# Layer 0 in another order (norm root, short convolution, diagonals), one more piece split ahead, and weight splits in steps of 1024 columns

## The chip, the cores and the metric

The kernel runs on one core of one Trainium2 chip. The metric is the time of one execution on the device in microseconds (us). PE is TensorE (matrix products), DVE is VectorE, ACT is ScalarE, POOL is GpSimd and SP is SyncE, whose queue issues the transfers (DMAs).

## What is computed

Two transformer-like blocks are applied to 256 tokens of 1024 channels, in float32. The first has an even layer (called layer 0 here) and an odd layer, the second a recurrent layer and a gated feed-forward. Layer 0, cut to what matters here:

```
z = h @ w_in;  va, vg, ga, xb, gb = split(z)
u   = depthwise_conv31(va * sigmoid(vg))          # "conv", 8 groups of 128 channels
y_a = silu(layernorm(u)) * silu(ga)
v   = depthwise_conv4(xb)                         # the short convolution
gr, gi = per-head products of v with w_r, w_i     # both directions
h_t = a_t * h_(t-1) + bx_t                        # linear recurrence, forward and backward
y_b = (h_forward + h_backward) * silu(gb)
x   = x + gate * (concat(y_a, y_b) @ w_out)
```

Each layer is preceded by a norm and by a scale and shift that come from a conditioning vector.

## The kernel before, in words

**Weights.** A piece of weights is a tile of 128 x 2048 floats (1 MB). SP loads it into one of 11 slots of the pool `w`. A product in float32 is made of three passes over two halves of lower precision: high x high, high x low and low x high (lines 365 to 367 with 256 or 512 tokens and columns, 413 to 415 with the weights as the moving side). ScalarE casts the high half of a piece (line 317) and VectorE subtracts it from the piece, which gives the low half (line 318). `halves` does that in steps of SW columns. `load_ahead(n_raw, n_split)` keeps 4 pieces loaded and LS = 2 split ahead of the one in use; where a layer's output rows take their last piece, `piece(last=True)` asks for LSB pieces instead, so LSB says how many pieces of the next layer are to be split before the residual and the norm between the layers.

**Order.** Layer 0's work is a table of names (`L0`): `glu`, `sh` and `cv` are the 31-tap convolution of a group, `xb`, `rb` and `gb` the recurrence's input, output rows and gate, `ga` and `co` the convolution's gate and output, `ln` its norm, `md` and `ml` the conditioning products (line 548, VectorE's sums line 507). The framework schedules the instructions of each engine from priorities which follow the order in which the code is written; on the chip each engine then runs its list strictly in order.

**Names used below.** `features(k)` (lines 771 to 774) makes the input of layer 0: VectorE xa, ScalarE hh, VectorE the low half. `shift` (line 901) copies a group's signal four times into the tile `four`, by four DMAs. `conv` makes a tile of diagonals `dg` on VectorE (line 908), which `order_after(..., tables["low"])` keeps behind the instruction held there, and multiplies `four` by it (line 915). `lru_in` makes the short convolution: ScalarE the third tap (j = 2, line 962), then VectorE three taps j = 0, 1, 3 for each of two heads q (line 968, tile `u`); the products of `u` with the gates' weights are line 372 (two of the four pieces xb use the three-pass form instead). ScalarE's gates, line 999 (`asq`) and VectorE's lines 996, 1000 and 1013 to 1019 (the scans) follow. `conv_norm` (lines 1024 to 1047) centres the convolution's result, sums its squares on TensorE (line 1042), and takes the root: VectorE line 445, POOL a power, VectorE and ScalarE two diagonals (lines 435 and 436), TensorE line 439, and a copy of it to `rsl`.

Of the kernel before, what the change touches and what calls it, by code (L numbers as in the profile page):

```python
# [8 lines left out]
F32 = mybir.dt.float32  # L9
# [3 lines left out]
ALU = mybir.AluOpType  # L13
# [4 lines left out]
MB = (6, 0)  # L18
MLATE = 0
TAIL = 400  # L20
LSB = 2
FENCE0 = -1
NT2 = 8
EARLY = (1, 1)
# [4 lines left out]
DIRECT = ('gv', 'so')  # L29
HOLD = ((), (), ())  # L30
LATE = [0, 2000, 600, 0]
SW = 512
SW_FROM = 0
START = [('w', 17), ('l', 4), ('x', 0), ('a', 0), ('y', 0), ('k', 0), ('w', 1), ('q', 0), ('w', 4), ('s', 0), ('f', 0), ('z', 0), ('r', 0), ('S', 0), ('a', 1), ('l', 2), ('k', 1), ('Z', 0), ('q', 1), ('f', 1), ('R', 0), ('a', 2), ('l', 2), ('r', 1), ('k', 2), ('q', 2), ('f', 2), ('s', 1), ('z', 1), ('R', 1), ('a', 3), ('l', 2), ('r', 2), ('k', 3), ('S', 1), ('Z', 1), ('q', 3), ('f', 3), ('R', 2), ('a', 4), ('l', 2), ('r', 3), ('k', 4), ('q', 4), ('f', 4), ('s', 2), ('z', 2), ('R', 3), ('a', 5), ('l', 2), ('r', 4), ('k', 5), ('S', 2), ('Z', 2), ('q', 5), ('f', 5), ('R', 4), ('a', 6), ('l', 2), ('r', 5), ('k', 6), ('q', 6), ('f', 6), ('s', 3), ('z', 3), ('R', 5), ('a', 7), ('l', 0), ('r', 6), ('k', 7), ('S', 3), ('Z', 3), ('q', 7), ('f', 7), ('R', 6), ('r', 7), ('R', 7), ('n', 1)]

# [12 lines left out]
]  # L48
# [42 lines left out]
T = 256  # L91
# [136 lines left out]
def build(tc, gates, wp, mp, vec, xT, cT, c2T, tok, cst, crow, out, dbg=None):  # L228
    nc = tc.nc
# [19 lines left out]
    def t1(name, shape=(P, T), dt=F32):  # L249
        return wk.tile(list(shape), dt, name=name, tag="t1", bufs=5)  # L250
# [246 lines left out]
    md = {}  # L497
# [218 lines left out]
    with ExitStack() as st0:  # L716
# [52 lines left out]
        def features(k):  # L769
            t = t1("xa")  # L770
            nc.vector.scalar_tensor_tensor(out=t, in0=X[:, k, :], scalar=A0[:, k, 0:1], in1=rsx, op0=ALU.mult, op1=ALU.mult)
            mod_shift(k)
            nc.scalar.activation(hx[0][:, k, :], t, AF.Identity, bias=S0[:, k, 0:1])
            nc.vector.scalar_tensor_tensor(out=hx[1][:, k, :], in0=t, scalar=S0[:, k, 0:1], in1=hx[0][:, k, :].bitcast(F32),
                                           op0=ALU.add, op1=ALU.subtract)

        def half_piece(s, g, low):

# [166 lines left out]
        def lru_in(m):  # L945

            gw = t4("gw", (P, 1024))
            nc.sync.dma_start(gw, gates[m])
            if m in GS:
                raw, gw = gw, [t4("gwh", (P, 1024), F32R), t4("gwl", (P, 1024), F32R)]  # L950
                split(*gw, raw)
            else:
                gw = [gw]
            pc = cut(piece(), k=KT)
            us, tiles = [], []
            bs = []
            for q in range(2):
                b = mm_bank()
                cols_both(b, pc, q)
                u = t2("u", (P, 2, T))  # L960
                h = 2 * m + q
                nc.scalar.activation(flat(u), b, AF.Identity, scale=v("ev_sconv_w", 16 + h), bias=v("ev_sconv_b", h))
                us.append(u)
                bs.append(b.rearrange("p (s t) -> p s t", s=2))
            for j in (0, 1, 3):
                o, i = (slice(2 - j, T), slice(0, T - 2 + j)) if j < 3 else (slice(0, T - 1), slice(1, T))
                for q in range(2):
                    nc.vector.scalar_tensor_tensor(out=us[q][:, :, o], in0=bs[q][:, :, i], scalar=v("ev_sconv_w", 8 * j + 2 * m + q),
                                                   in1=us[q][:, :, o], op0=ALU.mult, op1=ALU.add)
            for q in range(2):  # L970
                h = 2 * m + q
                us[q] = flat(us[q])
                rt, it, tt = (t4(n, (P, 2, 512)) for n in ("rt", "it", "tt"))
                tiles.append((rt, it, tt))
                up_ = [us[q]]
                if m in GS:
                    ut = t4("ut", (P, 2, 512), F32R)
                    up_ = [ut[:, i, :] for i in range(2)]
                    split(*up_, us[q])
                for d in range(2):  # L980
                    for w, (dst, bn) in enumerate(((rt, "ev_b_r"), (it, "ev_b_i"))):
                        g = side_bank()
                        o = (4 * q + 2 * d + w) * 128
                        mm_w(g, gw, up_, np.s_[:, o:o + 128], True, True)
                        act(dst[:, d, :], g, AF.Tanh, scale=0.5, bias=v(bn, 8 * d + h))
                for d in range(2):
                    act(tt[:, d, :], rt[:, d, :], AF.Tanh, scale=sp[:, 8 * d + h:8 * d + h + 1],
                        bias=sp[:, 8 * d + h:8 * d + h + 1])
            for q in range(2):
                h = 2 * m + q  # L990
                rt, it, tt = tiles[q]
                for d in range(2):
                    act(rt[:, d, :], rt[:, d, :], AF.Exp, scale=spn[:, 8 * d + h:8 * d + h + 1],
                        bias=spn[:, 8 * d + h:8 * d + h + 1])
                for d in range(2):
                    nc.vector.scalar_tensor_tensor(out=it[:, d, :], in0=it[:, d, :], scalar=1.0, in1=us[q],
                                                   op0=ALU.add, op1=ALU.mult)
                sq = t4("asq", (P, 2, 512))
                nc.scalar.activation(sq, rt, AF.Square)
                nc.vector.scalar_tensor_tensor(out=tt, in0=sq, scalar=1.0, in1=tt, op0=ALU.add, op1=ALU.mult)  # L1000
            lru[m] = tiles
# [22 lines left out]
        def conv_norm():  # L1024

            half = [cv[i // 2][:, 2 * (i % 2):2 * (i % 2) + 2, :] for i in range(4)]
            s4, s1 = t2("s4", (P, 2, T)), t1("s1")
            nc.vector.tensor_tensor(out=s4, in0=half[0], in1=half[1], op=ALU.add)
            for i in (2, 3):
                nc.vector.tensor_tensor(out=s4, in0=s4, in1=half[i], op=ALU.add)  # L1030
            nc.vector.tensor_tensor(out=s1, in0=s4[:, 0, :], in1=s4[:, 1, :], op=ALU.add)
            mu = ms_bank()
            nc.tensor.matmul(mu[:, 0:T], ones, s1, start=True, stop=True)
            va = ms_bank()
            for i in range(4):
                nc.vector.scalar_tensor_tensor(out=half[i], in0=mu[:, None, 0:T].to_broadcast([P, 2, T]), scalar=-1.0 / D, in1=half[i],
                                               op0=ALU.mult, op1=ALU.add)
                sq, s1 = t2("sq4", (P, 2, T)), t1("s1")
                nc.scalar.activation(sq, half[i], AF.Square)
                nc.vector.tensor_tensor(out=s1, in0=sq[:, 0, :], in1=sq[:, 1, :], op=ALU.add)  # L1040
                for j in range(2):
                    nc.tensor.matmul(va[:, j:j + 1], s1[:, 128 * j:128 * (j + 1)], ones[:, 0:1],
                                     start=i == 0 and j == 0, stop=i == 3 and j == 1)
            rsl = t1("rsl")
            nc.scalar.copy(rsl, rstd_of(va[:, 0:2], D, 1e-5))
            return rsl
# [17 lines left out]
        for name, m in L0:  # L1064
# [17 lines left out]
                ga_piece(m)  # L1082
            elif name == "ln":
                rsl = conv_norm()
            elif name == "co":
                conv_y[m] = conv_out(m, rsl)
            else:
# [484 lines left out]
```

## Time and profile before

| | |
|---|---|
| Time, median of 3 runs | 922.4 us (921.48 to 922.65) |
| The profiled execution | 922.77 us |
| Its span, first to last instruction | 920.6 us |
| PE busy | 896.4 us, 97% of the span |
| DVE busy | 673.2 us, 73% |
| ACT busy | 540.7 us, 59% |
| POOL busy | 14.6 us, 2% |

The span is what the trace shows; 2.2 us of the execution lie outside it. A busy share is an average over many stages, and an engine that is busy 73% of the time can still be the one that is waited for in one of them.

### The profile page before, as it was taken

What the parts mean: (1) busy time and instruction counts of PE and PEld (TensorE: products, weight loads), DVE (VectorE), ACT (ScalarE), POOL (GpSimd) and SP (SyncE); (2) the same over time, 40 slices, a digit from 0 to 9 for tenths busy, and PEclk for the clock granted to TensorE, in tenths of its full rate; (3) what the DMA queues carried; (4) which work ended last, traced back from release to release, by engine and by line L of the source; (5) the groups of instructions that cost most, each with busy time, mean ns of one, the idle gap of its engine ahead of it and who ended that gap; (6) DMA issues with size and microseconds to landing.
All of it is one profiled execution on the core that took longest, in us unless ns stands there. A gap on an engine that the chain in (4) does not pass through costs nothing.

```text
span 920.6 us, 16648 instructions
## 1 busy us (share of the span) xinstructions
PE 896.4 (97%) x6770; PEld 805.8 (88%) x6770; DVE 673.2 (73%) x1273; ACT 540.7 (59%) x986; POOL 14.6 (2%) x26
## 2 busy tenths in 40 slices
PE   8999999899999989999999999999999999999996
PEld 6876887586889889999999898999999999898896
DVE  3589696967776896968874544999688977756644
ACT  4444879686775555546573335972674865645542
POOL 1000000000000000000000000000000000000000
PEclk9999999999999989999999999999999999999999
DMA  9969484154667765674641752355666467555511
GB/s 365 416 218 366 157 302 152 61 206 137 244 246 303 296 225 201 224 235 163 255 138 61 302 188 92 138 184 205 240 225 247 150 218 251 205 183 184 183 46 46
DMA packets 32172, 190.05 MB, mean 206 GB/s; under 512 B 3584, under 2 KB 8064, under 8 KB 10976
## 3 DMA queue, kind: packets, MB, share of 16 engines
q1 hardware_dynamic: 31536, 186.50, 56.7%
q0 software_dynamic: 560, 2.49, 0.7%
q8 instruction: 53, 0.87, 0.4%
q14 instruction: 23, 0.19, 0.1%
HBM read 183.28 MB, written 1.05 MB: 200 GB/s over the span
## 4 chain that ended last, share of the span: by engine, by line
PE 87%; ACT 5%; DVE 5%; DMA 1%; issue 1%; POOL 0%; DVEq 0%; SPq 0%; POOLq 0%; ACTq 0%
PE mm L365 12%; PE mm L367 12%; PE mm L366 12%; PE mm L394 9%; PE acc L365 7%; PE acc L366 7%; PE acc L367 7%; PE mm L395 4%; PE acc L915 2%; PE acc L795 2%; PE ms L548 2%; PE acc L640 1%; PE ms L678 1%; ACT L300 1%; PE mm L413 1%; PE mm L414 1%
## 5 line engine op out<-in xcount | busy, mean ns | idle before, releaser
L318 DVE TENSOR_TENSOR w<-w 128x512 fp32r<-128x512 f32 x460 | 298.0, 684 | 81.2 <-ACT w L317 75.8
L317 ACT CAST w<-w 128x512 fp32r<-128x512 f32 x460 | 256.0, 618 | 100.0 <-PE mm L366 20.6
L367 PE MATMUL mm<-hh,w 128*128 128x256 f32 (+1 forms) x784 | 238.0, 304 | 2.9 <-DVE w L318 2.9
L365 PE MATMUL mm<-hh,w 128*128 128x256 f32 (+1 forms) x784 | 238.8, 305 | 1.0 <-ACT w L317 1.0
L366 PE MATMUL mm<-hh,w 128*128 128x256 f32 (+1 forms) x784 | 236.9, 302 | 0.0
L365 PEld LDWEIGHTS mm<-hh,w 128*128 128x128 f32 x784 | 149.5, 191 | 14.0 <-issue 5.1
L367 PEld LDWEIGHTS mm<-hh,w 128*128 128x128 f32 x784 | 149.2, 190 | 9.9 <-DVE w L318 3.5
L366 PEld LDWEIGHTS mm<-hh,w 128*128 128x128 f32 x784 | 149.5, 191 | 8.0 <-issue 2.3
L394 PE MATMUL mm<-hh,w 128*128 128x512 f32 x336 | 118.8, 397 | 0.0
L395 PE MATMUL mm<-hh,w 128*128 128x256 f32 x336 | 94.2, 281 | 0.0
L394 PEld LDWEIGHTS mm<-hh,w 128*128 128x128 f32 x336 | 63.2, 188 | 14.7
L395 PEld LDWEIGHTS mm<-hh,w 128*128 128x128 f32 x336 | 63.8, 190 | 0.0
L507 DVE SCALAR_TENSOR_TENSOR w<-w,crow 128x1024 f32<-128x1024 f32 x40 | 47.8, 1220 | 20.8 <-DMA w<-in_mp 20.7
L366 PE MATMUL acc<-fl,w 128*128 128x256 f32 x176 | 49.7, 283 | 0.0
L367 PE MATMUL acc<-fh,w 128*128 128x256 f32 x176 | 49.6, 283 | 0.0
L365 PE MATMUL acc<-fh,w 128*128 128x256 f32 x176 | 49.4, 284 | 0.0
L366 PE MATMUL acc<-yl,w 128*128 128x256 f32 x128 | 37.2, 290 | 0.0
L367 PE MATMUL acc<-yh,w 128*128 128x256 f32 x128 | 36.8, 288 | 0.0
L365 PE MATMUL acc<-yh,w 128*128 128x256 f32 x128 | 36.8, 287 | 0.0
L366 PE MATMUL acc<-zl,w 128*128 128x256 f32 x128 | 36.3, 284 | 0.0
L367 PE MATMUL acc<-zh,w 128*128 128x256 f32 x128 | 36.2, 283 | 0.0
L365 PE MATMUL acc<-zh,w 128*128 128x256 f32 x128 | 36.2, 283 | 0.0
(344 smaller groups left out, 1715.5 us busy)
## 6 DMA issues: line engine op xcount, KB each, us to landing
w<-in_wp SPq DMA_DIRECT2D x115, 1024.0 KB, 5.0
w<-in_mp SPq DMA_DIRECT2D x48, 1024.0 KB, 6.7
four<-up SPq DMA_DIRECT2D x32, 142.0 KB, 4.2
w<-in_wp SPq DMA_DIRECT2D x8, 512.0 KB, 10.7
gw<-in_gates SPq DMA_DIRECT2D x4, 512.0 KB, 4.9
X<-in_xT SPq DMA_DIRECT2D x1, 1024.0 KB, 5.0
ct<-in_cT SPq DMA_DIRECT2D x2, 512.0 KB, 9.3
crow<-in_crow SPq DMA_DIRECT2D x2, 512.0 KB, 10.7
```

The costliest lines, as they stand in the source:

```text
L300: i = nc.scalar.activation(out, in_, func, **kw).ins
L317: a = nc.scalar.copy(hi, src).ins
L318: return a, nc.vector.tensor_tensor(out=lo, in0=src, in1=hi.bitcast(F32), op=ALU.subtract).ins
L365: nc.tensor.matmul(o, wh, xh, start=start, stop=False)
L366: nc.tensor.matmul(o, wh, xl, start=False, stop=False)
L367: nc.tensor.matmul(o, wl, xh, start=False, stop=stop)
L394: nc.tensor.matmul(b, w[0][:, k, c], HH[:, :, 0, k, 0:T], start=k == 0, stop=False)
L395: nc.tensor.matmul(b[:, 0:T], w[1][:, k, c], HH[:, 0, 0, k, 0:T], start=False, stop=k == KT - 1)
L507: nc.vector.scalar_tensor_tensor(out=w[:, i, :], in0=w[:, i, :], scalar=1.0, in1=s, op0=ALU.mult, op1=ALU.mult, accum_out=o[:, 2 * c + i, :])
L548: nc.tensor.matmul(pm[32 * j:32 * (j + 1), :], s[:, k, :], w[:, 512 * j:512 * (j + 1)], start=c == 0, stop=c == chunks - 1)
L795: nc.tensor.matmul(acc_of(acc[g], i), w[wp_][:, k % 4, 128 * i:128 * (i + 1)], hx[hp][:, k, :], start=k == 0 and i % 2 == 0 and wp_ + hp = ...
L915: nc.tensor.matmul(b[32 * i:32 * (i + 1), 0:T], dg[:, j, i, :], four[:, i, o:o + T], start=j == 0, stop=j == n - 1)
```

## The change

Five edits, with no change to what is computed:

1. SW goes from 512 to 1024: each piece is split by two casts and two subtractions instead of four and four.
2. LSB goes from 2 to 3.
3. The root of the convolution's norm becomes a table entry of its own, `lb`, which stands behind `rb1` and `gb2`; `ln` keeps the centring and the sums of squares.
4. In the short convolution the loop over the heads q is now outside and the taps j inside, so all three taps of head 0 stand before those of head 1.
5. `tables["low"]` is now also set by the low halves of `features`, so the diagonals of the first convolution stand behind the last of them on VectorE.

```diff
-LSB = 2
+LSB = 3
...
-SW = 512
+SW = 1024
...
-    ('rb', 1), ('gb', 2), ('md', 1), ('xb', 3), ('md', 1), ('rb', 2), ('md', 1), ('gb', 3), ('ga', 1), ('ga', 0),
+    ('rb', 1), ('gb', 2), ('lb', 0), ('md', 1), ('xb', 3), ('md', 1), ('rb', 2), ('md', 1), ('gb', 3), ('ga', 1), ('ga', 0),
...
-            nc.vector.scalar_tensor_tensor(out=hx[1][:, k, :], in0=t, scalar=S0[:, k, 0:1], in1=hx[0][:, k, :].bitcast(F32),
-                                           op0=ALU.add, op1=ALU.subtract)
+            tables["low"] = nc.vector.scalar_tensor_tensor(out=hx[1][:, k, :], in0=t, scalar=S0[:, k, 0:1],
+                                                           in1=hx[0][:, k, :].bitcast(F32), op0=ALU.add, op1=ALU.subtract).ins
...
-            for j in (0, 1, 3):
-                o, i = (slice(2 - j, T), slice(0, T - 2 + j)) if j < 3 else (slice(0, T - 1), slice(1, T))
-                for q in range(2):
+            for q in range(2):
+                for j in (0, 1, 3):
+                    o, i = (slice(2 - j, T), slice(0, T - 2 + j)) if j < 3 else (slice(0, T - 1), slice(1, T))
...
+            return va
+
+        def conv_root(va):
             rsl = t1("rsl")
             nc.scalar.copy(rsl, rstd_of(va[:, 0:2], D, 1e-5))
             return rsl
...
+            elif name == "lb":
+                rsl = conv_root(rsl)
```

On VectorE, at the end of the features: the diagonals `dg_642` of the first convolution (`dg_638` after the change) and the last features' xa, hh. Before:

```order
L490 SCALAR_TENSOR_TENSOR A0_103<-ms_481,V_68,b1_101 128x2
L908 TENSOR_TENSOR dg_642<-C_72,V_68 128x896
L771 SCALAR_TENSOR_TENSOR xa_509<-X_70,A0_103,rs_161 128x256
L495 TENSOR_SCALAR S0_104<-ms_481,V_68 128x2
L847 MEMSET sm_575 128x16
L774 SCALAR_TENSOR_TENSOR hh_67<-xa_509,S0_104,hh_67 128x256
L318 TENSOR_TENSOR w_559<-w_550,w_558 128x512 x4
```

Now:

```order
L490 SCALAR_TENSOR_TENSOR A0_103<-ms_481,V_68,b1_101 128x2
L771 SCALAR_TENSOR_TENSOR xa_509<-X_70,A0_103,rs_161 128x256
L495 TENSOR_SCALAR S0_104<-ms_481,V_68 128x2
L847 MEMSET sm_571 128x16
L774 SCALAR_TENSOR_TENSOR hh_67<-xa_509,S0_104,hh_67 128x256
L908 TENSOR_TENSOR dg_638<-C_72,V_68 128x896
L318 TENSOR_TENSOR w_559<-w_550,w_558 128x1024 x2
```

The diagonals moved behind xa and the low half of hh, and the split of `w_559` has two steps in place of four.

On TensorE, where the fourth convolution (`acc_838`, now `acc_830`, with the tile `four_722`, now `four_718`) begins. The rows ahead of each fence's first are products of the piece `mm_979`, now `mm_967`. Before:

```order
L439 MATMUL ms_883<-dg_880,ones_73 128x128 x2
L548 MATMUL ms_920<-w_918,S_81 32x512
L915 MATMUL acc_838<-four_722,dg_836 32x256 x3
L548 MATMUL ms_920<-w_918,S_81 32x512 x3
L548 MATMUL ms_920<-w_961,S_81 32x512
```

Now:

```order
L915 MATMUL acc_830<-four_718,dg_828 32x256
L439 MATMUL ms_875<-dg_872,ones_73 128x128
L915 MATMUL acc_830<-four_718,dg_828 32x256
L439 MATMUL ms_875<-dg_872,ones_73 128x128
L548 MATMUL ms_912<-w_910,S_81 32x512
L915 MATMUL acc_830<-four_718,dg_828 32x256 x30
```

The convolution now begins ahead of the norm product of line 439, and its first two matmuls stand apart. Ahead of it, 17 matmuls of `mm_967` stand behind line 612's, where before 12 of `mm_979` did. Further up, the first convolution stood behind 50 matmuls of the two pieces before it, and stands behind 35 now.

On VectorE, at the short convolution of the third piece xb (`u_1813` before, `u_1773` after). `w_1975`, `w_2031` and, before, `w_2030` are low halves of pieces to come. Before:

```order
L1018 TENSOR_TENSOR hsum_1686<-tt_1565 128x256
L1019 TENSOR_TENSOR sb_1684<-sb_1684,hsum_1686 128x512
L922 SCALAR_TENSOR_TENSOR cv1_616<-up1_618,V_68,cv1_616 128x256 x2
L318 TENSOR_TENSOR yl_1699<-sb_1684,yh_1698 128x512
L922 SCALAR_TENSOR_TENSOR cv1_616<-up1_618,V_68,cv1_616 128x256
L968 SCALAR_TENSOR_TENSOR u_1813<-mm_1788,V_68,u_1813 128x2x254
L922 SCALAR_TENSOR_TENSOR cv1_616<-up1_618,V_68,cv1_616 128x256
L968 SCALAR_TENSOR_TENSOR u_1813<-mm_1788,V_68,u_1813 128x2x255 x2
L318 TENSOR_TENSOR w_2030<-w_1776,w_2029 128x512 x2
```

Now:

```order
L1018 TENSOR_TENSOR hsum_1650<-tt_1533 128x256
L922 SCALAR_TENSOR_TENSOR cv1_612<-up1_614,V_68,cv1_612 128x256
L1019 TENSOR_TENSOR sb_1648<-sb_1648,hsum_1650 128x512
L922 SCALAR_TENSOR_TENSOR cv1_612<-up1_614,V_68,cv1_612 128x256
L318 TENSOR_TENSOR w_1975<-w_1740,w_1974 128x1024
L318 TENSOR_TENSOR yl_1663<-sb_1648,yh_1662 128x512
L922 SCALAR_TENSOR_TENSOR cv1_612<-up1_614,V_68,cv1_612 128x256
L968 SCALAR_TENSOR_TENSOR u_1773<-mm_1748,V_68,u_1773 128x2x254
L968 SCALAR_TENSOR_TENSOR u_1773<-mm_1748,V_68,u_1773 128x2x255
L318 TENSOR_TENSOR w_2031<-w_1860,w_2030 128x1024
L968 SCALAR_TENSOR_TENSOR u_1773<-mm_1748,V_68,u_1773 128x2x255
```

Ahead of the third tap of head 0 there now stand one step of 1024 columns (`w_1975`) and, between the second tap and the third, a second one (`w_2031`); before, no step of a weight split stood between the scans and the third tap. Higher up, behind the second set of diagonals, one step of 1024 columns of `w_1975` takes the place of one of 512 of `w_1903`.

## Rows read from the trace of the kernel before

**Rows 1.** Page of the profile, part 1: busy time of each engine, its share, instructions.

```profile
PE 896.4 (97%) x6770; PEld 805.8 (88%) x6770; DVE 673.2 (73%) x1273; ACT 540.7 (59%) x986; POOL 14.6 (2%) x26
```

**Rows 2.** Busy time by stretch: from:to, length, PE, PEld, DVE, ACT, POOL, PEclk, DMA.

```profile
171.00:180.00 9.00, 6.59 (x25) 3.16 (x26) 8.77 (x15) 5.40 (x8) 1.93 (x3) 1.00 0.38 131
320.00:326.20 6.20, 4.13 (x33) 3.73 (x31) 6.20 (x12) 4.26 (x10) 0.00 (x0) 1.00 0.72 263
326.20:333.00 6.80, 6.18 (x29) 6.18 (x30) 6.80 (x12) 2.31 (x6) 0.00 (x0) 0.50 0.67 236
```

**Rows 3.** Groups by line and shape, VectorE: count, busy us, mean ns, idle before.

```profile
L318 DVE TENSOR_TENSOR w<-w 128x512 fp32r<-128x512 f32 x460 | 298.0, 684 | 81.2 <-ACT w L317 75.8 <-issue 2.0 <-PE acc L366 1.6
```

**Rows 4.** Groups by line and shape, ScalarE.

```profile
L317 ACT CAST w<-w 128x512 fp32r<-128x512 f32 x460 | 256.0, 618 | 100.0 <-PE mm L366 20.6 <-issue 18.1 <-PE mm L394 17.1
```

**Rows 5.** Line 786 (a low half made in 1024 columns): min/median/max ns.

```profile
L786 DVE TENSOR_TENSOR w<-w x9: 685/1225/1226, 14.8 to 45.6; 128x1024 fp32r<-128x1024 f32 x7, 128x512 fp32r<-128x512 f32 x2
```

**Rows 6.** Line 789 (a high half made in 1024 columns).

```profile
L789 ACT CAST w<-w x9: 620/1030/1053, 12.0 to 44.5; 128x1024 fp32r<-128x1024 f32 x7, 128x512 fp32r<-128x512 f32 x2
```

**Rows 7.** TensorE in order of time: start, us, line, tiles, [idle before].

```profile
49.09 1.15 PE L795 MATMUL acc<-hh,w 128*128 128x256 f32 x7 [1.13 <-ACT hh L773]
...
74.43 0.68 PE L439 MATMUL ms<-dg,ones 128*128 128x128 f32 x4 [0.30 <-DVE dg L435]
...
76.61 0.62 PE L915 MATMUL acc<-four,dg 128*32 128x256 f32 x2 [0.52 <-DMA four<-up]
...
170.60 0.39 PE L367 MATMUL mm<-hh,w 128*128 128x512 f32 x1
173.41 3.67 PE L372 MATMUL acc<-u,gw 128*128 128x512 f32 x8 [2.42 <-issue]
177.02 1.06 PE L548 MATMUL ms<-w,S 128*32 128x512 f32 x6
...
203.04 0.68 PE L439 MATMUL ms<-dg,ones 128*128 128x128 f32 x4 [1.02 <-DVE dg L435]
...
246.28 0.38 PE L367 MATMUL mm<-hh,w 128*128 128x256 f32 x1 [1.18 <-DVE w L318]
...
307.22 0.95 PE L556 MATMUL ms<-C,row 128*128 128x4 f32 x8
...
324.76 0.38 PE L365 MATMUL mm<-hh,w 128*128 128x256 f32 x1 [1.02 <-ACT w L317]
326.82 0.58 PE L367 MATMUL mm<-hh,w 128*128 128x256 f32 x1 [1.67 <-DVE w L318]
...
569.48 0.39 PE L414 MATMUL mm<-w,hh 128*128 128x256 f32 x1 [1.13 <-DVE w L318]
...
576.03 0.39 PE L414 MATMUL mm<-w,hh 128*128 128x256 f32 x1 [0.57 <-DVE w L318]
...
601.69 0.43 PE L1365 MATMUL acc<-lx,st 128*128 128x64 f32 x2 [0.49 <-DVE st L1376]
```

**Rows 8.** VectorE in order of time.

```profile
46.89 1.08 DVE L908 TENSOR_TENSOR dg<-C,V 128x896 f32<-128x896 f32 x1
47.89 0.48 DVE L771 SCALAR_TENSOR_TENSOR xa<-X,A,rs 128x256 f32<-128x256 f32 x1
...
155.25 1.23 DVE L1000 SCALAR_TENSOR_TENSOR tt<-asq,tt 128x1024 f32<-128x1024 f32 x1 [5.19 <-ACT asq L999]
...
157.52 1.22 DVE L1000 SCALAR_TENSOR_TENSOR tt<-asq,tt 128x1024 f32<-128x1024 f32 x1
...
160.26 1.22 DVE L1013 TENSOR_TENSOR it<-it,tt 128x1024 f32<-128x1024 f32 x1
...
171.79 1.52 DVE L968 SCALAR_TENSOR_TENSOR u<-mm,V,u 128x510 f32<-128x510 f32 x2
```

**Rows 9.** Transfer issues between 53.5 and 54.4 us: count, KB, us to landing.

```profile
four<-up SPq DMA_DIRECT2D x1, 142.0 KB, 2.8
```

**Rows 10.** Transfer issues between 69 and 69.9 us.

```profile
four<-up SPq DMA_DIRECT2D x2, 142.0 KB, 7.3
```

## The prediction

> **What bounds the kernel now.** I read the page first: TensorE is busy for 896 of 920.6 us, VectorE for 73% and ScalarE for 59% [rows 1]. So only what lets TensorE stand, or slows its clock, can move the end. Then the waits of TensorE in order of time, which give the places where another engine is late [rows 7]. They are few: 1.13 us for the last features, 0.30 and 0.52 us around the fourth convolution, 2.42 us for the short convolution of the third piece xb, 1.02 us for the root's diagonals, 1.18 us for a low half, 1.02 and 1.67 us at the start of layer 1, and in the recurrent layer 1.13, 0.57 and 0.49 us, with some smaller ones. Then the windows with the granted clock: from 326.2 to 333.0 us it is 0.50, that is 1.2 in place of 2.4 GHz, right behind the two waits of 2.69 us in sum; around the single wait of 2.42 us it stays at 1.00 [rows 2, 7]. TensorE's 6.18 busy us in that stretch would have been 3.09 at the full clock, so the slow stretch costs about 3.1 us.
>
> A difference under 0.2% (1.8 us) cannot be told from no change here.
>
> **Steps of 1024 columns.** 460 subtractions of 684 ns and 460 casts of 618 ns [rows 3, 4] become 230 each of 1225 and 1030 ns [rows 5, 6]. Instructions of one VectorE queue overlap by 0.08 us (the diagonals run from 46.89 for 1.08 us, the next starts at 47.89 [rows 8]), so in a full queue a step of 512 takes 0.60 us and one of 1024 takes 1.145: 0.06 us saved a pair, some 14 us over the kernel. On ScalarE it is at most 206 ns a pair. Neither engine ends the chain, so the price of this is zero where TensorE has work. It is not zero where TensorE waits for a half: the first columns of a piece come 0.54 us later, and an urgent instruction that finds a step ahead of it waits for 1.145 instead of 0.60 us.
>
> **The features and the convolutions (36 to 87 us).** The diagonals stood ahead of xa and took 1.00 us of the queue [rows 8]. Behind them stood xa, then ScalarE's hh, and TensorE waited 1.13 us for hh [rows 7]. Now they stand behind the low half of hh: -1.0. But the first convolution now comes after 35 matmuls in place of 50, 1.8 us earlier in its row, while its four copies land 2.8 us after issue each [rows 9] and can start only about 0.85 us earlier, since they need the sums that TensorE has just got earlier. The four land one after the other over 2.1 us; with eight matmuls between them to fill, I take a wait of 0.9. The fourth convolution's copies stand in SP's queue behind two loads of 1 MB; before, they landed 7.3 us after issue [rows 10], and TensorE waited 0.52 us for them and 0.30 just ahead for the norm's diagonals [rows 7]. The loads can be issued about 1.9 us earlier now, as the first convolution ends earlier. TensorE is about 1.3 us earlier at the sums of squares (line 612); then 17 matmuls follow where 12 did, and the norm product and line 548, which stood ahead of the convolution (1.7 us from 74.43 to the wait before 76.61), stand behind its first matmul. I estimate a wait of 1.5 in place of 0.82, and 0.2 for the single matmuls between products of another form. Sum: -1.0 + 0.9 + 0.7 + 0.2 = **+0.8**, between -1.1 (the copies land in time) and +2.0.
>
> **The short convolution of the third xb (155 to 178 us).** VectorE's queue is full here from 155.25 us to the end of the third tap (171.79 + 1.52 = 173.31), and TensorE starts the gates' products 0.1 us later, at 173.41 [rows 8, 7]. The heads' new order takes head 1's taps out from between head 0's, which gives little, as only head 0's stood there. What counts is what the scheduler put in. (a) The gate products of the second xb stand behind 12 more matmuls, so the last of them comes 1.4 us later; ScalarE was about 0.4 behind, so asq and line 1000 come 1.0 later than 155.25. (b) ScalarE has a cast of 1030 ns in place of 618 between the two asq: +0.4 for the second line 1000, which started at 157.52 [rows 4, 6, 8]. (c) The step of w_1975 behind the diagonals is 0.54 longer. So line 1013 begins 1.9 us later than 160.26. (d) From there the queue is the same up to the third tap, but for two steps of 1024 columns: +2.29. The third tap ends at about 173.31 + 1.9 + 2.3 = 177.5, and TensorE starts line 372 at 177.6. TensorE's own row ahead has three more products of line 548 (about 1.0 us by [rows 7], 177.02) and the four of line 556 (0.9 us for four); so it stands for about 177.6 - 172.0 - 0.85 = 4.75 us in place of 2.42: **+2.3**. The lower bound is 0 (ScalarE not later, and the steps filled by other waits), the upper 3.5.
>
> **The clock behind that wait.** Of the waits seen here, 2.42 us alone did not lower the granted clock, and 1.02 + 1.67 us with 0.3 of work between did [rows 2, 7]. A stand of 3.2 us, then line 556, then 1.5 us is longer than either. I take the lower clock at three chances in four, and its price as at 326.2 us: **+3.1**.
>
> The Trainium skill (TensorE: Matmul & The Clock Gate, section on HAM oscillation) says that a wait for data that is long enough lets the array's clock fall, so that the work behind it starts cold, and counts half of the cold time as lost. This trace agrees with the fall; by the page's half the 6.8 us cost 3.4 where the rows say 3.1, and the sum would be 0.3 higher in the case with one more fall.
>
> **The root (202 us).** Line 439 now stands behind all of `rb1` and of `gb2`, and one matmul more, while line 445 and the power start as soon as the sums are there. TensorE reaches it about as late as the diagonals are ready: the wait of 1.02 goes, **-1.0** (bounds -1.0 and +0.5).
>
> **Behind gb3 (245 us).** The low half that TensorE waited 1.18 us for stood on VectorE behind the scans; now both its steps stand ahead of line 1000. It goes; the next late thing is the recurrence's y for `rb3`, which then comes some 0.5 us after TensorE. **-0.7** (-1.2 to +0.5).
>
> **The start of layer 1 (323 us).** With LSB = 3, the second piece u is split before the residual, where VectorE and ScalarE stand. But the gate's piece that TensorE waited for is the third. Its cast is 1030 ns, so the wait of 1.02 becomes about 1.5; its low half still stands behind four sums of line 507 and ends its first step at about 325.6, where TensorE comes at 325.4: 1.75 in place of 2.69, **-1.0** (-2.5 to +1). A wait of that length did not lower the clock at 173 us, so I give six chances in ten that the 3.1 us of the slow stretch go too: **-3.1**. If they do not, the gain is only the 1.0.
>
> **The recurrent layer (566 to 605 us).** The first wait for a low half grows by 0.54, as its first step is 1024 columns. The wait of 0.57 for the last quarter of it goes, and 0.12 beside it. Then VectorE reaches the products `ke`, `kc` and the states later by two or three half steps each, and TensorE's row has been filled with more matmuls ahead: I estimate +0.5, +0.4 and +0.6 on waits that were 0.2 to 0.5 us [rows 7]. **+1.3**, between -0.7 and +2.5. Elsewhere (90 to 155, 340 to 540, from 660 on) TensorE has no wait that a half could shorten, and the queues of the other two engines have room.
>
> **The sum.** 0.8 + 2.3 - 1.0 - 0.7 - 1.0 + 1.3 = +1.7. The slow clock goes from 326 to 177 us: -3.1 + 3.1. Against the profiled execution's 922.77 that is 924.5; it ran 0.4 above the median, so I forecast **924.1** (own range 922 to 926).
>
> **Rivals.**
> 1. The slow clock comes at both places (the two waits at 324 us still suffice): 924.1 + 3.1 = 927.2. For it: the waits stay in the same pattern. Against: they are shorter.
> 2. It comes at neither: 921.0. For it: the stand at 172 us is cut in two by line 556. Against: 3.2 us alone is longer than anything that left the clock up here.
> 3. On the other side: `u` is not later. This is decided by whether TensorE has line 372's input by about 175.5 us: then it stands for 2.6 us, the clock stays, and the gains at 202, 245 and 324 us remain: 924.1 - 2.3 - 3.1 = 918.7. For it: (a) and (b) are estimates on ScalarE, whose queue had idle room just before 155.25 (VectorE stood 5.19 us [rows 8]). Against: the two steps of 1.145 us are in the row whatever ScalarE does.
> 4. The waits change places and nothing else, as the halves are made well ahead: 922.4.
>
> **Chances.** Forecast 0.40, rival 1 0.18, rival 2 0.17, rival 3 0.20, rival 4 0.05. With about 2 us of spread in each sum, faster by over 0.2% (below 920.6): 0.02 + 0 + 0.08 + 0.17 = 0.27; slower (above 924.2): 0.19 + 0.17 + 0.01 = 0.37; the rest, 0.36, within 0.2%. The range from 918 to 927.5 leaves out the outer parts of rivals 1 and 3.
>
> **What the profile after would show.** The wait of line 795 for hh near 47.7 us is under 0.2; line 915 has waits for `four` near 56 and 73 us; line 372 starts at 177 to 178 us behind 4 to 5 us of standing, with a granted clock of 0.50 behind it; line 439 near 204 us does not wait; the wait near 245 us is gone; at 324 us two waits sum to under 2 us and the clock is 1.00 from 326 to 333. The forecast is wrong if line 372 starts by 176 us, if 0.50 stands behind the waits at 324 us, or if a wait of over 1 us turns up in a stretch that I call free.

## The result and the profile after: slower by 1.2%

The changed kernel took **933.33 us** (median of 4 executions, 932.29 to 935.93), the kernel before 921.94 (4 executions beside it, 920.49 to 922.65). The ratio is 1.0121, with a 95% interval of 1.009 to 1.0152: slower by 11.4 us, where 924.1 was forecast with a range up to 927.5. The profiled execution took 935.93 us with a span of 934.2.

Of the page of the changed kernel, part 1, and from part 5 the groups of the two steps that the change doubled:

```profile
PE 905.2 (97%) x6770; PEld 806.4 (86%) x6770; DVE 660.0 (71%) x1043; ACT 519.4 (56%) x756; POOL 15.7 (2%) x26
...
L318 DVE TENSOR_TENSOR w<-w 128x1024 fp32r<-128x1024 f32 x230 | 277.2, 1220 | 99.9 <-ACT w L317 94.0
L317 ACT CAST w<-w 128x1024 fp32r<-128x1024 f32 x230 | 233.6, 1047 | 124.3 <-PE mm L366 28.4
```

Against [rows 1, 3, 4] the two engines that make the halves did get quicker: VectorE is busy for 13 us less and ScalarE for 21 us less. TensorE, which bounds the kernel, is busy for 9 us more with the same 6770 matmuls. So work was saved where time was to spare, and time was lost where there was none.

TensorE's waits in the changed kernel, summed by what it waited for (total, times, longest):

```profile
PE ms L556 <- ACT row L552: 3.5, 1, 3.5
PE ms L740 <- DVE xsq L735: 3.4, 1, 3.4
PE acc L915 <- DMA four<-up: 2.7, 3, 1.9
PE mm L414 <- DVE w L318: 1.7, 1, 1.7
PE mm L365 <- ACT w L317: 1.4, 1, 1.4
PE acc L365 <- ACT ut L317: 1.4, 1, 1.4
...
PE ms L1290 <- DVE ke L1342: 1.0, 1, 1.0
PE acc L795 <- ACT hh L773: 0.9, 2, 0.6
PE acc L372 <- DVE u L968: 0.7, 1, 0.7
PE acc L365 <- ACT yh L317: 0.5, 1, 0.5
```

Gone or smaller against [rows 7] are the waits for the last `hh` (1.13), for the root's diagonals (1.02), for the low half near 246 us (1.18) and the second of the two at the start of layer 1 (1.67). New or longer are those for `four` (2.7 in place of 0.52), for `ut` (1.4, none before), for `row` and `u` in one place (3.5 + 0.7 in place of 2.42), for `ke` and for `yh`. Line 414 waits for 1.7 us in one place, before in two (1.13 and 0.57).

The windows of the changed kernel (columns as in [rows 2]) show where the clock fell, that is went from 2.4 to 1.2 GHz (PEclk 0.50):

```profile
10.90:14.30 3.40, 3.40 (x22) 1.64 (x20) 0.00 (x0) 0.89 (x2) 0.00 (x0) 0.51 1.00 411
...
79.20:82.60 3.40, 3.40 (x12) 1.40 (x14) 0.19 (x1) 0.00 (x0) 0.00 (x0) 0.50 0.90 262
...
185.00:191.80 6.80, 6.10 (x14) 3.40 (x14) 5.38 (x9) 1.99 (x3) 1.42 (x3) 0.50 0.33 136
...
341.70:348.50 6.80, 6.80 (x60) 6.80 (x59) 6.80 (x9) 2.23 (x3) 0.00 (x0) 1.00 0.91 313
```

The slow stretch behind the waits of layer 1 [rows 2] is gone (layer 1 starts 15.5 us later here, so the last window is the same stretch of work). Three others have come: 3.4 us in the opening stretch, behind the wait for `xsq`; 3.4 us behind the wait for `four`; and 6.8 us behind the wait for `row`. TensorE in order of time at three of the new waits:

```profile
79.04 0.88 PE L915 MATMUL acc<-four,dg 128*32 128x256 f32 x2 [1.86 <-DMA four<-up]
...
148.55 0.50 PE L365 MATMUL acc<-ut,gwh 128*128 128x512 f32 x1 [1.44 <-ACT ut L317]
...
184.73 1.64 PE L556 MATMUL ms<-C,row 128*128 128x8 f32 x8 [3.48 <-ACT row L552]
187.07 1.22 PE L372 MATMUL acc<-u,gw 128*128 128x512 f32 x1 [0.70 <-DVE u L968]
```

VectorE, and under it ScalarE, of the changed kernel in order of time ahead of that last place:

```profile
180.57 0.69 DVE L1019 TENSOR_TENSOR sb<-sb,hsum 128x512 f32<-128x512 f32 x1
181.17 0.48 DVE L922 SCALAR_TENSOR_TENSOR cv<-up,V,cv 128x256 f32<-128x256 f32 x1
181.56 1.22 DVE L318 TENSOR_TENSOR w<-w 128x1024 fp32r<-128x1024 f32 x1
182.70 0.69 DVE L318 TENSOR_TENSOR yl<-sb,yh 128x512 fp32r<-128x512 f32 x1
183.30 0.48 DVE L922 SCALAR_TENSOR_TENSOR cv<-up,V,cv 128x256 f32<-128x256 f32 x1
183.70 1.53 DVE L968 SCALAR_TENSOR_TENSOR u<-mm,V,u 128x508 f32<-128x508 f32 x2
185.14 1.22 DVE L318 TENSOR_TENSOR w<-w 128x1024 fp32r<-128x1024 f32 x1
186.27 1.40 DVE L968 SCALAR_TENSOR_TENSOR u<-mm,V,u 128x510 f32<-128x510 f32 x2
```

```profile
181.29 0.62 ACT L317 CAST yh<-sb 128x512 fp32r<-128x512 f32 x1 [5.34 <-DVE sb L1019]
181.81 0.77 ACT L962 ACTIVATE u<-mm,V 128x512 f32<-128x512 f32 x1
182.49 1.03 ACT L317 CAST w<-w 128x1024 fp32r<-128x1024 f32 x1
183.42 0.78 ACT L962 ACTIVATE u<-mm,V 128x512 f32<-128x512 f32 x1
184.09 0.58 ACT L552 COPY row<-ms 128x512 f32<-128x512 f32 x1
```

This is how a full queue hands lateness on. VectorE reaches `sb` at 180.57; ScalarE stands for 5.34 us until it has it, because `yh` is next in its row; behind `yh` stand two `u`, a long cast and only then the copy of `row`, which TensorE's line 556 needs. On VectorE two steps of 1024 columns stand between `sb` and the third tap. TensorE is at line 556 at 181.25 and has `u` at 187.07.

Where the 13.6 us between the two spans lie, from the starts of the matmuls that have the same count on TensorE's row in both profiled executions (the order differs a little, so single places are right to some tenths):

| place on TensorE's row | after - before, us | forecast |
|---|---|---|
| opening stretch (wait for `xsq` 3.4 in place of 1.5, then a slow clock) | +2.9 | none |
| last features (`hh`) | -0.9 | -1.0 |
| the convolutions and the norm behind them | +5.3 | +1.8 |
| gates of the second xb (`ut`) | +2.1 | 0 |
| `row` and `u` of the third xb, with the clock behind them | +4.8 | +5.4 |
| root | -0.9 | -1.0 |
| behind gb3 | +2.2 | -0.7 |
| start of layer 1, with the clock behind it | -4.1 | -4.1 |
| rest of layer 1 | +0.8 | 0 |
| recurrent layer | +0.1 | +1.3 |
| everything behind it | +1.2 | 0 |

The opening stretch belongs to this execution more than to the change: the wait for `xsq` was 0.9 to 3.4 us over all the profiles, with 2.6 and 2.2 us in the first two kernels below.

### The profile page after: what moved, and what is told of

Its sections match the earlier page's. It is cut to its first block, busy times and chain, and to the rows that moved or that the text cites. A ratio compares the mean times of both kernels' runs of the same rounds, so it can differ in the third digit from the quotient of the medians.

```text
span 934.2 us, 16180 instructions
## 1 busy us (share of the span) xinstructions
PE 905.2 (97%) x6770; PEld 806.4 (86%) x6770; DVE 660.0 (71%) x1043; ACT 519.4 (56%) x756; POOL 15.7 (2%) x26
## 4 chain that ended last, share of the span: by engine, by line
PE 75%; DVE 12%; ACT 7%; issue 2%; DMA 2%; SPq 0%; POOL 0%; DVEq 0%; ACTq 0%; POOLq 0%
PE mm L365 10%; PE mm L367 10%; PE mm L366 10%; PE mm L394 8%; PE acc L365 6%; PE acc L366 6%; PE acc L367 6%; PE mm L395 4%; DVE w L318 2%; PE ms L548 2%; PE acc L795 2%; DMA four<-up 1%; ACT w L317 1%; PE acc L915 1%; ACT rt L300 1%
## 5 line engine op out<-in xcount | busy, mean ns | idle before, releaser
L318 DVE TENSOR_TENSOR w<-w 128x1024 fp32r<-128x1024 f32 x230 | 277.2, 1220 | 99.9 <-ACT w L317 94.0
L317 ACT CAST w<-w 128x1024 fp32r<-128x1024 f32 x230 | 233.6, 1047 | 124.3 <-PE mm L366 28.4
## 6 DMA issues: line engine op xcount, KB each, us to landing
crow<-in_crow SPq DMA_DIRECT2D x2, 512.0 KB, 10.2
```

The lines of the kernel that those rows point to most:

```text
L317: a = nc.scalar.copy(hi, src).ins
L318: return a, nc.vector.tensor_tensor(out=lo, in0=src, in1=hi.bitcast(F32), op=ALU.subtract).ins
```

## The experiments

My theory was that the doubled steps made the loss: VectorE and ScalarE work in order, so whatever stands behind a step of 1024 columns comes later, and the scheduler lays its rows out around the long steps. The rival was that the reordering of layer 0 made it (convolutions closer to their copies, root and taps in another place). A second rival was TensorE itself: the scheduler pulled apart line 548's groups of four matmuls, and each single one costs nearly as much as four.

### 1. Each part alone

The doubled steps in the kernel before, with nothing else:

```diff
-SW = 512
+SW = 1024
```

> The kernel before with weight splits in steps of 1024 columns and nothing else. Theory 1 (the long steps are the cause): VectorE and ScalarE run their lists in order, so an urgent instruction behind a step waits for 1.1 us instead of 0.6, and the scheduler lays the rows out for longer steps; nearly all of the loss of 11 us is here, +9 to +14 us, with waits of TensorE at the fourth convolution, at the gates of the second and third xb, and a granted clock of 0.50 behind at least one of them. Theory 2 (the new place of the root and of the diagonals is the cause): within 2 us of the kernel before.

The rest of the change, with the steps of 512 columns:

```diff
-SW = 1024
+SW = 512
```

> The changed kernel with the steps put back to 512 columns; the order of layer 0 and the third piece split ahead stay. Theory 1: faster than the kernel before by 1 to 5 us, since the waits at the last features and at the root go (1.0 us each) and the start of layer 1 gains what the third piece gives. Theory 2: slower by 6 to 11 us.

The kernel before with three pieces of layer 1 split ahead, alone:

```diff
-LSB = 2
+LSB = 3
```

> The kernel before with three pieces split ahead of a layer's end and nothing else. If the pieces split ahead are what took the two waits at 324 us down in the changed kernel, they shrink here too and the granted clock stays at 1.00 from 326 to 333 us: -2 to -5 us. If it was the longer step that did it (fewer steps behind the sums of line 507), the waits stay as before and the time within 1 us.

The kernel before with the root's own entry in the list, the taps by head, and the diagonals behind the low half, but with LSB = 2 and 512 columns (edits 3, 4 and 5 of the change, shortened here):

```diff
-    ('rb', 1), ('gb', 2), ('md', 1), ('xb', 3),
+    ('rb', 1), ('gb', 2), ('lb', 0), ('md', 1), ('xb', 3),
...
-            nc.vector.scalar_tensor_tensor(out=hx[1][:, k, :], in0=t, scalar=S0[:, k, 0:1], in1=hx[0][:, k, :].bitcast(F32),
+            tables["low"] = nc.vector.scalar_tensor_tensor(out=hx[1][:, k, :], in0=t, scalar=S0[:, k, 0:1],
...
-            for j in (0, 1, 3):
+            for q in range(2):
+                for j in (0, 1, 3):
```

> The kernel before with the new place of the root, the short convolution by heads and the diagonals behind the features; steps of 512, two pieces ahead. Theory 1: the waits of 1.13 us at the last features and of 1.02 us at the root go and nothing comes instead, -1 to -2.5 us. Theory 2: slower by 5 to 11 us, with waits in the convolutions.

Measured: steps of 1024 alone **936.58 us, ratio 1.015** (1.0114 to 1.0185); the whole change with 512 **918.88 us, 0.9963** (0.9946 to 0.998); three pieces ahead 920.95, 0.9998 (0.9975 to 1.0021); the reordering 922.41, 0.9996 (0.9978 to 1.0014). So the sign is settled: the doubled steps cost 1.5%, and all the rest of the change gains 0.4%, neither half of it measurable alone. Two gains that I had expected did not show: 2 to 5 us from three pieces ahead, though its second wait at the start of layer 1 shrank from 1.67 to 1.07 us, and 1 to 2.5 us from the reordering, though its waits for `hh` and at the root went. The version with 512 columns beats both kernels. TensorE's waits in it:

```profile
PE acc L372 <- issue: 2.4, 1, 2.4
...
PE mm L365 <- ACT w L317: 1.0, 1, 1.0
...
PE acc L915 <- DMA four<-up: 0.6, 1, 0.6
```

Line 556's wait for `row` and the wait for `ut` are not in its list, `u` is late by the same 2.4 us as before, and `four` by 0.6. With the steps of 1024 alone `row`, `u` and `ut` are late, in a kernel that has none of the reordering; the wait at the fourth convolution, which I had expected there too, is only 0.4 us (TensorE's waits, steps of 1024 in the kernel before):

```profile
PE ms L556 <- ACT row L552: 3.5, 1, 3.5
...
PE acc L372 <- DVE u L968: 1.9, 1, 1.9
...
PE acc L365 <- ACT ut L317: 1.4, 1, 1.4
...
PE acc L915 <- DMA four<-up: 0.4, 1, 0.4
```

The wait for `row` is 3.5 us in each kernel that has long steps on both engines in layer 0 (this one, the changed one, and two below), and in none of the others.

### 2. Which steps, and on which engine

Steps of 512 columns in the 28 pieces of layer 0 whose kinds are named here, 1024 in the others (the edits of this section are shortened):

```diff
-    halves(raws[i], SW if i > SW_FROM else 2048)
+    halves(raws[i], (512 if i < 4 + sum(name in ("glu","xb","gb","ga","rb","ra") for name, _ in L0) else SW) if i > SW_FROM else 2048)
```

> The changed kernel with steps of 512 columns for the 28 pieces of layer 0 and of 1024 for all others. Theory 1a (the long steps cost time only where TensorE waits for VectorE and ScalarE, in layer 0): the gates of the second and third xb and the fourth convolution wait as in the kernel before, so about 919 to 922 us, 0 to 2 us above the version with 512 everywhere. Theory 1b (the long steps cost something in every stage): 924 us or more.

The changed kernel with ScalarE's casts in 512 columns and VectorE's subtractions in 1024 (for each step two casts, then one subtraction):

```diff
-nc.scalar.copy(hi[:, c:c + 1024], raw[:, c:c + 1024])
+for d in (0, 512):
+    nc.scalar.copy(hi[:, c + d:c + d + 512], raw[:, c + d:c + d + 512])
```

> The changed kernel with ScalarE's casts in steps of 512 and only VectorE's subtractions in steps of 1024. If ScalarE's long casts delay the halves and the gates (the low half can only start when both casts are done, so this does not help the first columns), the waits at the gates of the second xb shrink: 925 to 930 us. If it is VectorE's long subtraction ahead of u and the low halves: 931 to 935 us.

The reverse, casts in 1024 and subtractions in 512:

```diff
-nc.vector.tensor_tensor(out=lo[:, c:c + 1024], in0=raw[:, c:c + 1024], in1=hi[:, c:c + 1024], op=ALU.subtract)
+for d in (0, 512):
+    nc.vector.tensor_tensor(out=lo[:, c + d:c + d + 512], in0=raw[:, c + d:c + d + 512],
+                            in1=hi[:, c + d:c + d + 512], op=ALU.subtract)
```

> The changed kernel with VectorE's subtractions in steps of 512 behind ScalarE's casts in steps of 1024. If VectorE's long step ahead of urgent work is what costs (u, ke, the low halves): 922 to 927 us. If it is ScalarE's long cast ahead of the gates and of the first columns: 930 to 934 us.

Measured: 512 in layer 0 only, 922.84 us, 1.0013 (0.9999 to 1.0027); short casts 930.26, **1.0091** (1.0064 to 1.0118); short subtractions 920.26, **0.9986** (0.997 to 1.0002). Of the 1.58% between 0.9963 and 1.0121, making only VectorE's steps short gives back 1.35, only ScalarE's 0.30. So it is VectorE's subtraction, although the cast is the step that comes first. The run with short casts alone would not have decided it: its 930.26 us lie between the ranges of its two theories. The run with short subtractions came out better than its better range (922 to 927). In TensorE's waits with short subtractions (lines are numbered 3 higher here, so line 372 is L375) the whole place of `row` and `u` is down to 1.4 us, and the 1.4 for `ut` is gone:

```profile
PE acc L375 <- ACT row L555: 1.4, 1, 1.4
```

VectorE's row at the third xb shows what became of the two long steps there (short subtractions, third tap of head 0):

```profile
172.91 1.53 DVE L971 SCALAR_TENSOR_TENSOR u<-mm,V,u 128x510 f32<-128x510 f32 x2
174.35 1.28 DVE L330 TENSOR_TENSOR w<-w 128x512 fp32r<-128x512 f32 x2
```

The splits stand behind the third tap, as in the kernel before; none stands between `sb` (169.33 us) and it. So at this place the long steps did not cost the 0.54 us by which each is longer, but two whole steps that the scheduler put ahead of urgent work.

With short casts `row` and `u` are still late, by 4.6 us in sum:

```profile
PE acc L375 <- DVE u L971: 2.4, 1, 2.4
PE ms L559 <- ACT row L555: 2.2, 1, 2.2
```

Steps of 1024 outside layer 0 still cost some 4 us (922.84 against 918.88), between what the two theories said: in layer 0 the waits are nearly those with 512 throughout, but the profile shows the two waits at the start of layer 1 at 1.44 and 1.06 us, where the version with 512 throughout has 1.01 and less than 0.1. The clock also fell twice in that profile, for 3.4 us each, and not once within the other, so part of the 4 us can be the clock.

### 3. The diagonals

The changed kernel without the edit that lets the diagonals of the convolutions wait for the low half of the features:

```diff
-            tables["low"] = nc.vector.scalar_tensor_tensor(out=hx[1][:, k, :], in0=t, scalar=S0[:, k, 0:1],
-                                                           in1=hx[0][:, k, :].bitcast(F32), op0=ALU.add, op1=ALU.subtract).ins
+            nc.vector.scalar_tensor_tensor(out=hx[1][:, k, :], in0=t, scalar=S0[:, k, 0:1], in1=hx[0][:, k, :].bitcast(F32),
+                                           op0=ALU.add, op1=ALU.subtract)
```

> The changed kernel with the diagonals of the first convolution back ahead of the last features. If the two edits act together (the diagonals' place lets the scheduler put the first convolution after 35 products instead of 42 to 50, where its copies have not landed), the wait of 1.9 us at the fourth convolution and the slow clock behind it go, the wait of 1.1 us at the features comes back: 929 to 931 us, faster than the changed kernel by 2 to 4 us. If the edits only add up: 934 us, slower by the 1.0 us of the features.

Measured: 928.41 us, 1.0073 (1.0052 to 1.0094). With long steps this edit, which takes 0.9 us from the features, costs 5 us net. In the profile without it the first convolution comes after 42 matmuls in place of 35, `four` is waited for once, for 0.3 us, the clock does not fall at 79 us, and the wait of 1.15 us for `hh` is back. The same edit is in the version with 512 columns, where the wait for `four` is 0.6 us and no slow clock follows. So the price of this edit shows only beside the long steps. The other edits weigh more beside them too: from the kernel with long steps alone (936.58) to this one, which has edits 2 to 4 as well, it is 8.2 us less, where with 512 columns those edits were worth 3 us together with the diagonals. The median clock rose from 0.990 to 0.994 between the two, so a part of the 8.2 us can be the clock; which of the edits does the rest was not tried.

### 4. Line 548 taken apart, and kept together

Line 548 is four matmuls of 32 columns, one for each column group. In the version with 512 columns, priorities were set so that other matmuls come between the four (52 groups on TensorE's row in place of 26):

```diff
             for j in range(4):
+                tc.cur_priority += 40 * (j > 0)
                 nc.tensor.matmul(
```

> The version with 512 everywhere and all the rest of the change, with the second to fourth matmul of each conditioning chunk (line 548, four column groups of 32) put 40 places later, so that TensorE's row has 52 groups of them in place of 26. If the four run side by side when they stand together (four took 1.0 us in the trace, a single one 1.0 us as well), 26 more groups cost 10 to 20 us: 928 to 938 us. If each costs its quarter wherever it stands: 918 to 921 us.

And so that the four stay together, in the version with 512 columns, in the changed kernel and in the kernel before:

```diff
             for j in range(4):
+                tc.cur_priority -= 400 * (j == 1)
                 nc.tensor.matmul(
```

> The version with 512 everywhere and all the rest of the change, with the second to fourth matmul of each conditioning chunk moved up, so that the four always stand together: 20 groups in TensorE's row in place of 26. If a group costs 0.92 us whatever its size, as 26 more groups cost about 24 us, six fewer save 5 to 6 us: 912 to 915 us, faster than the kernel before by about 1%. If only groups that were moved out of place cost so much: 917 to 920 us.

> The changed kernel (steps of 1024) with the four matmuls of each chunk always together: 20 groups in place of 29. If a part of what the change lost is that its order cuts these groups, 9 fewer save 7 to 9 us: 924 to 927 us; what is left above the version with 512 and whole groups (some 11 us) is then the waits and the slow clock. If the groups matter only where TensorE has no wait beside them: 929 to 933 us.

> The kernel before with the four matmuls of each chunk always together (20 groups in place of 25) and nothing else: 4 to 5 us faster, 916 to 918 us, if a group costs 0.92 us; within 1 us of before if not.

Measured: apart 942.15 us, **1.0224** (1.0201 to 1.0247), 23.3 us above the version it was made from. TensorE's group of line 548 (by line; an added line makes it L549 in the second) with 512 columns, and taken apart:

```profile
L548 PE MATMUL ms<-w,S 128*32 128x512 f32 x160 | 25.6, 601 | 0.0
...
L549 PE MATMUL ms<-w,S 128*32 128x512 f32 x160 | 45.4, 602 | 0.0
```

The same 160 instructions (two for each of 80 matmuls) of the same mean length keep TensorE busy for 19.8 us more, 0.76 us for each of 26 more groups: the four run side by side, and a single one takes as long as four. Single rows show it too. Four matmuls in the kernel before, and one alone in the changed kernel:

```profile
251.02 1.06 PE L548 MATMUL ms<-w,S 128*32 128x512 f32 x8
...
256.05 1.05 PE L548 MATMUL ms<-w,S 128*32 128x512 f32 x2
```

The kernel's time rose by more than the 10 to 20 us that I had expected. The changed kernel has 29 groups and 27.3 us:

```profile
L548 PE MATMUL ms<-w,S 128*32 128x512 f32 x160 | 27.3, 602 | 0.0
```

Before, it was 24.5 us. So 2.8 us of the loss are in this line (the lower clock may have part in them), and 1.1 of these are in the version with 512 columns too (25.6), which is faster than the kernel before. Kept together, the groups give the changed kernel about 4 us back, 929.49 and 1.007 (1.0047 to 1.0092), and it is still slow: `row` is still waited for by 3.5 us. The 4 us (7 to 9 were expected) are not all this rival's share, since the edit also joins groups that were apart in the kernel before; its share is the 2.8 us, a quarter of the loss. The other two gain nothing, where 5 to 6 and 4 to 5 us were expected if every group cost the same: 921.53, 0.9982 (0.9962 to 1.0002) with 512 columns, 924.38, 1.0028 (1.0014 to 1.0042) in the kernel before. The line itself is busy for 21.1 us in both, but the wait for `u` is 3.6 us in place of 2.4, with the clock at 0.50 behind it (10.2 and 3.4 us), and `ut` is waited for by 0.9 us: the groups pushed other work in TensorE's row.

## Why the prediction was wrong, step by step

**Steps of 1024 columns.** The saving was sized right (14 us forecast on VectorE, 13.2 measured). The step that failed is the sentence that the price "is zero where TensorE has work" and that "elsewhere (90 to 155, 340 to 540, from 660 on)" no wait could arise. I looked for waits that were there before and asked how each would change; longer steps in in-order queues also make waits where there were none. `ut` at 148.55 us is such a case: 1.44 us (and 0.22 for its low half) in a stretch that I had called free, which I had named as one of the things that would make the forecast wrong. It is a chain over both engines (ScalarE, then VectorE, of the changed kernel):

```profile
142.77 2.00 ACT L317 CAST w<-w 128x1024 fp32r<-128x1024 f32 x2 [2.30 <-DVE w L318]
144.67 0.78 ACT L962 ACTIVATE u<-mm,V 128x512 f32<-128x512 f32 x1
145.48 2.31 DVE L968 SCALAR_TENSOR_TENSOR u<-mm,V,u 128x508 f32<-128x508 f32 x3 [2.79 <-ACT u L962]
```

ScalarE's two long casts wait for VectorE's long subtractions, ScalarE's third tap stands behind the casts, and VectorE then waits for that tap. With short subtractions ScalarE's order is the same and VectorE stands for 2.78 us, but its splits between `hsum` and that stand are four steps of 512 columns in place of three of 1024, the chain starts earlier, and only the low half of `ut` is waited for, by 0.2 us. Together the places called free gave +4.1 us (2.1 + 0.8 + 1.2).

**The convolutions.** Forecast +1.8 behind the features' -1.0, measured +5.3. The waits for `four` were sized well: 0.71 and 0.16 us where I took 0.9, then 1.86 where I took 1.5 with the diagonals. Two things were missing from the term. The first is the clock: I asked whether it falls at 177 and at 326 us, and not here, where 1.86 us of standing was followed by 3.4 us at 0.50; with TensorE busy throughout, that is 1.7 us lost. The second are the single matmuls of other forms, among them those of line 548: I priced them at 0.2; what is left of the +5.3 without the waits (+1.9) and the clock (+1.7) is 1.7, an estimate by difference. Experiment 3 shows that this term comes from the edit and the long steps together.

**The third xb.** Forecast +2.3 for the wait and +3.1 for the clock, measured +4.8 together. TensorE stood for 3.48 + 0.70 = 4.18 us in two parts (4.75 forecast), and the clock was at 0.50 for 6.8 us, of which 6.10 were busy. The two steps of 1024 columns that I had counted in VectorE's row are there, at 181.56 and 185.14. The order was as forecast too, a long stand ahead of line 556 and a shorter one behind it; that `row` waits for ScalarE, which waits for VectorE's `sb`, is how one late queue made both. Line 372 starts at 187.07 where 177 to 178 was forecast, but TensorE is 9.4 us late by then from the places ahead, so the forecast of this place itself held.

**Root and features** came as forecast (-0.9 each).

**Behind gb3.** Forecast -0.7, measured +2.2. The wait of 1.18 us went, and one of 0.5 for `yh` came, as I had said. What was missing is again line 548: before, it stands here in four groups of four; now, in groups of 1, 3, 1, 1, 2, 4 and 4. Three more groups at 0.76 us are 2.3 us by experiment 4.

**Start of layer 1.** Forecast -1.0 and -3.1, measured -4.1. The first wait became 1.44 us (1.5 forecast) and the second went away. The run with LSB = 3 alone has both in another size (1.02 and 1.07) and its time is that of the kernel before, so a good part of this gain is the clock, which does not fall in every execution (below).

**Recurrent layer.** The wait for line 414 was as forecast (1.66), that for `ke` too (1.0), but the sum was +0.1 in place of +1.3: the others shrank by as much.

Put together: the waits that I had forecast came to within a microsecond, and the step that failed is the price of nothing for every other place. The loss I did not see, some 9 us in this profile without the opening stretch (13.6 - 2.9 against the forecast's 1.7), lies in new waits in stretches without any, in a clock that fell at one more place, and in TensorE's own row, which the scheduler laid out worse. The runs settle that most of it comes with VectorE's long subtractions (experiment 2). What stays open is how much of it is the queue itself (a step of 1.22 us ahead of something urgent) and how much is the scheduler's other order: a kernel with long steps and the order of the short ones was not tried. The traces with short subtractions point both ways. At the third xb the order went back with the length (experiment 2). At the first convolution it stayed near the changed kernel's (37 matmuls ahead, against 35), and the waits for `four` were 0.2 us in sum all the same.

## What to carry to other kernels

Before making an off-path instruction longer, look at who stands behind it in its in-order queue at every place, not only at places that already wait: an engine that is 73% busy on average had no time to spare where several consumers were just in time, and the steps that saved 13 us of its work cost some 14 us of the kernel's (933.33 against 918.88). Look also at what a scheduler puts ahead of urgent work once the instruction is longer. When an edit and a change of size come together, run each alone: here the rest of the change was worth 0.4% and the size took it back four times over. And count groups of matmuls that run side by side as one: where a scheduler pulls them apart, each piece costs nearly as much as the whole.

## What the runs showed of the hardware

**Column groups.** Four matmuls of 32 columns in a row took some 1.0 us on TensorE and a single one nearly as much: 26 groups more cost 19.8 us of busy time and 23.3 us of the kernel's.

**The clock does not follow the length of a wait alone.** The kernel with the reordering alone has the same two waits at 324 us as the kernel before, 1.02 and 1.68 us against 1.02 and 1.67 [rows 7], and its clock stayed up (TensorE in order of time, and the window behind):

```profile
324.02 0.38 PE L365 MATMUL mm<-hh,w 128*128 128x256 f32 x1 [1.02 <-ACT w L317]
326.08 0.39 PE L367 MATMUL mm<-hh,w 128*128 128x256 f32 x1 [1.68 <-DVE w L318]
```

```profile
326.20:333.00 6.80, 6.80 (x58) 6.80 (x59) 6.80 (x12) 2.29 (x5) 0.00 (x0) 1.00 0.63 206
```

Before, the same stretch ran at 0.50 [rows 2]. In the other direction, the wait of 2.42 us for `u` left the clock up in the kernel before, and in the kernel with 512 columns in layer 0 only the clock fell behind it (TensorE in order of time, and the window behind it):

```profile
172.05 5.37 PE L372 MATMUL acc<-u,gw 128*128 128x512 f32 x8 [2.42 <-issue]
```

```profile
173.00:176.70 3.70, 3.70 (x6) 1.51 (x5) 3.31 (x6) 1.63 (x3) 0.14 (x1) 0.54 0.29 120
```

The same eight matmuls took 5.37 us there and 3.67 before [rows 7]. The clock also goes with most of the spread between executions of one kernel: of 25 executions of the kernel before that ran beside the first four experiments, the three with a mean granted clock of 0.999 took 919.25 to 921.39 us, the four with 0.992 took 924.65 to 925.64. The changed kernel's executions had 0.990 to 0.995. By these figures (5 us for 0.007) the lower clock, 0.993 in the median against 0.997, makes about 3 of the 11.4 us, as an estimate (whatever else differs between executions at those clocks is in it); the rest are waits and the groups of line 548. The Trainium skill (TensorE: Matmul & The Clock Gate, the section on HAM oscillation) ties a fall of the clock to waits; in the profiles read here every fall within the kernel comes in or behind a wait, so they agree; they also show that a wait of the same length is followed by a fall in one profile and not in another, so a forecast can price it only by chance times cost.
